# Query and key operands of a hybrid decoder layer: split once over 128 rows, then carried to their rows by transfers

## Chip, core and metric

The kernel runs on one core of one Trainium2 chip. The metric is the device time of one execution in microseconds (us). The core has a matrix engine (TensorE, PE in the profile; PEld is its weight load), a vector engine (VectorE, DVE), a scalar engine (ScalarE, ACT), a general engine (GpSimd, POOL) and a sync engine (SyncE, SP) that here only issues transfers. Every engine works through its own queue of instructions in order and waits on semaphores; transfers (DMA) are issued by an instruction of SP, POOL or ACT and land later.

## What is computed

One inference step of a decoder layer for a prompt of 1024 tokens and 8 decode sequences of 8 tokens (1088 columns in all), with shared weights. Cut to what matters here:

```python
xn = rmsnorm(x, norm1_g)
proj = xn @ w_in
q, k, v, glu_a, glu_b, gate_a, gate_b = split(proj)
attn = sliding_window_attention(q, k, v, sinks)      # window 128, 16 heads over 4 key heads, head size 64
branch_a = attn @ w_o_attn
branch_b = silu(layernorm(causal_dwconv31(glu_a * sigmoid(glu_b)))) @ w_pb
h = x + (sigmoid(gate_a) * branch_a + sigmoid(gate_b) * branch_b) @ w_out
y = h + conv_ffn(rmsnorm(h))                          # then a final rmsnorm
```

Everything is float32 at the outside. Inside, each operand of a matmul is kept as two float32r halves, a rounded high half and the difference to it (low half), and a product is three matmuls: high by high, high by low, low by high.

## The kernel before

**Tiling.** Activations lie with channels on the 128 partitions and tokens along the row. A weight of 128 output channels is a "unit": `stream` (L204) runs it over three chunks of columns (384, 384 and 320; the last has 256 prompt columns and 64 decode columns). A chunk is 8 steps of three matmuls (L200, L201, L202), so 24 matmuls into one PSUM bank; there are four banks of tag `mm` and four of tag `aux`. After a chunk an evacuation function `evac(c, o, n, ps)` reads the bank. The order of the units is the list `SEQUENCE` (L54): `b a q0 g q0 b a q0 q0 k0 b a v v`, then gates, `b`s and `a`s, then `q1 q1 q1 g q1 k1 b a ...`. The first five units are run chunk by chunk side by side with the first normalisation (L832 to L848).

**Queries.** Units `q0` and `q1` hold two heads each (64 rows of one key head g=0, 64 of g=1); four units make a group of four heads for each g. The operand of the scores for key head g is the tile `q{g}` of 128 rows: the rows r of g hold the high half, the other 64 rows x hold the low half. So a single matmul over 128 rows multiplies both halves. `q_evac` (L715) does, per g, an ACT copy of 64 rows into r (L727) and a DVE subtraction of 64 rows into x (L728).

**Keys.** `do_k` (L737) makes `kd{g}` with the high half on both sets of 64 rows and `kl{g}` with the low half on both: per g, ACT writes kd's rows r (L748), DVE writes kl's rows r (L750), and ACT copies both to the rows x (L751, L752).

**Users.** `attn_unit` (L338) reads them in `scores` (L356, L357), for the first group after `v`, for the second from the moment that its keys are there. Its output is written over the columns of `q0`/`q1` that it has read; those of the first group are sent to DRAM by POOL (`attn_spill`, L400), and the second group's queries use the same two tiles (one buffer each).

**Other work beside it.** ACT and DVE split each raw weight into halves (`w_split`, L181 and L182), evacuate the `b`, `a` and gate units, do the softmax and the splits of its transposes (`split_ps`, L228 to L230), and DVE runs the 31-tap convolutions (`conv`, L468; its taps are L480, some 47 long DVE operations per convolution). SP loads raw weights (L158, two buffers `wraw`) and the convolution's history into `u` (L661, two buffers).

**What sets the order.** The code is traced by a framework that tracks reads and writes by region, puts in the semaphores, and orders each engine's queue ahead of time with its own estimates of durations, by priority among what it reckons to be ready. Priority is the order of tracing; `later(off)` lowers it, and the convolutions stand at `later(1200)` (L690), so they fill what DVE has left. At run time each queue is followed strictly. A tile of a pool has as many buffers as its `bufs`; the pools `qp`, `cv` and `gl` have one unless a call says otherwise.

Of the kernel before, what the change touches and what calls it, by code (L numbers as in the profile page):

```python
# [6 lines left out]
F32 = mybir.dt.float32  # L7
F32R = mybir.dt.float32r
AF = mybir.ActivationFunctionType
ALU = mybir.AluOpType  # L10
AX = mybir.AxisListType

P = 128
# [106 lines left out]
class Build:  # L120
# [515 lines left out]
    def pool(self, es, name, side="right", bufs=1):  # L636
        return es.enter_context(self.tc.tile_pool(name=name, bufs=bufs, side=side, reuse_waits="tile"))

    def phase_x(self):
        nc, tc, a, pool = self.nc, self.tc, self.a, self.pool  # L640
# [5 lines left out]
        gl = pool(right, "gl")  # L646
# [56 lines left out]
        def gate_evac(kind, i):  # L703
# [8 lines left out]
                nc.gpsimd.dma_start(dst[i, :, o:o + n], t[:, :n])  # L712
            return ev

        def q_evac(p, j):  # L715
            st = states[p]
            if j == 0:
                st["q"] = [self.t(qp, [P, 4, T], f"q{g}", F32R) for g in range(2)]
                st["qs"] = self.t(qp, [P, NB // 2, 3 * 8 * NT], "qs")
                nc.gpsimd.memset(st["qs"], 0.0)  # L720

            def ev(c, o, n, ps):
                m = min(n, SEQ - o)
                for g in range(2):
                    r, x = [slice(y * HD, (y + 1) * HD) for y in (g, 1 - g)]
                    q = st["q"][g][:, j, o:o + m]
                    nc.scalar.copy(q[r], ps[r, :m])  # L727
                    nc.vector.tensor_tensor(q[x], ps[r, :m], q[r].bitcast(F32), ALU.subtract)  # L728
                if m < n:
                    for g in range(2):  # L730
                        r = slice(g * HD, (g + 1) * HD)
                        row = st["qs"].rearrange("p a (s x) -> p a s x", s=3)[r, :, 0:3:2]
                        nc.scalar.copy(row[:, :, :, (4 * g + j) * NT:(4 * g + j + 1) * NT],
                                       ps[r, m:n].rearrange("p (a s t) -> p a s t", a=NB // 2, s=2))
            return ev

        def do_k(p):  # L737
            st = states[p]
            st["ks"] = self.t(kv, [P, NS], "ks")
            st["kd"] = [self.t(kv, [P, SEQ], f"kd{g}", F32R) for g in range(2)]  # L740
            st["kl"] = [self.t(kv, [P, SEQ], f"kl{g}", F32R) for g in range(2)]

            def ev(c, o, n, ps):
                m = min(n, SEQ - o)
                for g in range(2):
                    r, x = [slice(y * HD, (y + 1) * HD) for y in (g, 1 - g)]
                    kd = st["kd"][g][:, o:o + m]
                    nc.scalar.copy(kd[r], ps[r, :m])  # L748
                    kl = st["kl"][g][:, o:o + m]
                    nc.vector.tensor_tensor(kl[r], ps[r, :m], kd[r].bitcast(F32), ALU.subtract)  # L750
                    nc.scalar.copy(kd[x], ps[r, :m])  # L751
                    nc.scalar.copy(kl[x], kl[r].bitcast(F32))  # L752
                if m < n:
                    nc.scalar.copy(st["ks"], ps[:, m:n])
                    kf = self.t(gl, [P, 384], "gt", bufs=2)[:, :WIN]
                    nc.scalar.copy(kf, ps[:, m - WIN:m])
                    nc.gpsimd.dma_start(a["o_kp"][p], kf)
                    nc.gpsimd.dma_start(a["o_kn"][p], st["ks"])

            self.stream(("k", p), xs, ev)  # L760
# [38 lines left out]
        p0_es = ExitStack()  # L799
        p0 = pool(p0_es, "p0", "left")  # L800
        put_q = [q_evac(0, j) for j in range(2)]
        spare = [q[:, 3, :DM] for q in states[0]["q"]]
        self.slot = lambda i: (None, spare) if i == 4 else (p0, "xy"[i - 2]) if 2 <= i < FIRST else (self.wp, i % 2)
# [60 lines left out]
        for n, (kind, i) in enumerate(self.order[:self.n_in]):  # L864
# [16 lines left out]
            if kind == "b":  # L881
                u = do_b(i)
            elif kind == "a":
                do_a(i, u)
            elif kind in ("ga", "gb"):
                self.stream((kind, i), xs, gate_evac(kind, i))
            elif kind == "q":
                if i == (1, 0):
                    self.drain()
                self.stream((kind, i), xs, q_evac(*i))  # L890
            elif kind == "k":
                do_k(i)
                if i == 1:
                    plan_units(1)
            elif kind == "v":
                if i == 0:
                    do_v()
                    plan_units(0)
# [892 lines left out]
```

## Time and profile before

| | us |
|---|---|
| median of 3 runs | 1660.74 |
| lowest, highest | 1658.13, 1662.14 |
| the profiled execution's own time | 1659.53 |
| its span in the profile | 1657.8 |

In the profile, "busy" of PE counts the modelled length of a matmul, and matmuls overlap: a 384-column matmul is listed with about 0.33 us, but the next one starts well before that. The pace of PE is therefore read from the starts of neighbouring rows, and its stalls from the idle time that a row shows in brackets, `[idle before <-releaser]`. Rows of windows give, for each engine, the busy us and the number of instructions; "PEclk" is the granted clock of PE as a share of full speed. Rows of a line's view give minimum, median and maximum of its durations in ns.

### The profile page before, as it was taken

How to read it: one execution, taken by the hardware profiler on the slowest of the kernel's cores; microseconds unless marked ns; L12 is line 12 of the kernel's file. 1: busy time of each engine (PE TensorE's matmuls, PEld its weight loads, DVE VectorE, ACT ScalarE, POOL GpSimd, SP SyncE). 2: the span in 40 equal slices, each digit the busy share in tenths (PEclk: the TensorE clock that was granted, in tenths of full speed). 3: DMA queues.
4: the chain of work that ended last, by engine and by line, in shares of the span. 5: the costliest groups of instructions: out<-in, count | busy, mean ns of one | idle time of the engine just before them, and what ended most of it. 6: DMA issues, size and time to landing. Idle time of an engine off the chain costs nothing.

```text
span 1657.8 us, 30344 instructions
## 1 busy us (share of the span) xinstructions
PE 1642.9 (99%) x11616; PEld 1627.3 (98%) x11616; DVE 1336.1 (81%) x2430; ACT 893.3 (54%) x1817; POOL 328.1 (20%) x589
## 2 busy tenths in 40 slices
PE   9999999999999999999999999999999999999998
PEld 9999999999999999999999999999999999999997
DVE  8899999999769995866685897877777777977556
ACT  7434477753488754993343564444444446834322
POOL 1210114171211211110000123333433220000050
PEclk9999999999999999999999999999999999999999
DMA  6122216254421255545346527676777544857473
GB/s 213 43 52 71 60 63 167 62 178 103 115 67 47 83 195 184 165 137 190 113 136 194 134 79 204 183 182 176 182 176 176 144 112 149 286 157 218 138 148 117
DMA packets 121313, 232.12 MB, mean 140 GB/s; under 512 B 25408, under 2 KB 67536, under 8 KB 120736
## 3 DMA queue, kind: packets, MB, share of 16 engines
q1 hardware_dynamic: 88208, 140.14, 27.6%
q0 software_dynamic: 32384, 89.51, 21.3%
q8 instruction: 91, 1.49, 0.4%
q10 hardware_dynamic: 576, 0.53, 0.1%
q14 instruction: 54, 0.44, 0.1%
HBM read 169.74 MB, written 89.62 MB: 156 GB/s over the span
## 4 chain that ended last, share of the span: by engine, by line
PE 81%; DVE 11%; ACT 4%; issue 2%; DMA 1%; POOL 0%; SPq 0%; DVEq 0%; ACTq 0%; POOLq 0%
PE mm L200 19%; PE mm L202 19%; PE mm L201 19%; PE aux L200 6%; PE aux L202 6%; PE aux L201 6%; DVE c L480 3%; DVE bt L480 2%; PE aux L366 1%; ACT p L332 1%; ACT p L336 1%; PE aux L378 1%; DVE wlo L182 1%; PE aux L356 1%; PE aux L379 1%
## 5 line engine op out<-in xcount | busy, mean ns | idle before, releaser
L200 PE MATMUL mm<-xh,whi 128*128 128x384 f32 (+1 forms) x920 | 306.6, 333 | 0.6 <-ACT whi L181 0.6
L201 PE MATMUL mm<-xl,whi 128*128 128x384 f32 (+1 forms) x920 | 301.1, 327 | 0.0
L202 PE MATMUL mm<-xh,wlo 128*128 128x384 f32 (+1 forms) x920 | 300.7, 327 | 0.0
L200 PEld LDWEIGHTS mm<-xh,whi 128*128 128x128 f32 x920 | 173.3, 188 | 2.2 <-ACT whi L181 1.2
L201 PEld LDWEIGHTS mm<-xl,whi 128*128 128x128 f32 x920 | 173.4, 188 | 1.0
L202 PEld LDWEIGHTS mm<-xh,wlo 128*128 128x128 f32 x920 | 173.1, 188 | 0.1
L1209 DVE SCALAR_TENSOR_TENSOR acc<-st,fc,acc 128x1104 f32<-128x1104 f32 x88 | 119.5, 1361 | 8.7 <-ACT acc L1207 7.9
L181 ACT CAST whi<-wraw 128x1024 fp32r<-128x1024 f32 (+1 forms) x65 | 62.7, 970 | 56.8 <-PE mm L201 44.6
L480 DVE SCALAR_TENSOR_TENSOR bt<-u,consts,bt 128x513 f32<-128x513 f32 x120 | 89.7, 747 | 0.6
L480 DVE SCALAR_TENSOR_TENSOR c<-sm,hsum,c 128x512 f32<-128x512 f32 x120 | 89.4, 745 | 0.5
L182 DVE TENSOR_TENSOR wlo<-wraw,whi 128x1024 fp32r<-128x1024 f32 (+1 forms) x65 | 72.5, 1121 | 20.1 <-ACT whi L181 19.6
L480 DVE SCALAR_TENSOR_TENSOR c<-u,consts,c 128x512 f32<-128x512 f32 x112 | 83.5, 745 | 0.2
L229 ACT CAST wlo<-th 128x512 fp32r<-128x512 f32 x56 | 35.1, 626 | 65.0 <-PE aux L202 41.3
L1378 ACT COPY st<-mm 128x272 f32<-128x272 f32 (+2 forms) x133 | 44.4, 350 | 46.8 <-PE mm L202 46.8
L200 PE MATMUL mm<-th,whi 128*128 128x272 f32 x240 | 69.3, 289 | 0.0
L202 PE MATMUL mm<-th,whi 128*128 128x272 f32 x240 | 69.3, 289 | 0.0
L201 PE MATMUL mm<-tl,whi 128*128 128x272 f32 x240 | 69.1, 288 | 0.0
L332 ACT ACTIVATE p<-p,nm 128x257 f32<-128x257 f32 (+1 forms) x128 | 62.2, 490 | 11.0 <-DVE nm L327 10.1
L1357 DVE TENSOR_TENSOR st<-st,aux 128x272 f32<-128x272 f32 (+2 forms) x95 | 34.2, 378 | 38.5 <-PE aux L202 38.5
L202 PE MATMUL mm<-sh,wlo 128*128 128x384 f32 (+1 forms) x192 | 62.6, 326 | 0.0
L201 PE MATMUL mm<-sl,whi 128*128 128x384 f32 (+1 forms) x192 | 62.6, 326 | 0.0
L200 PE MATMUL mm<-sh,whi 128*128 128x384 f32 (+1 forms) x192 | 62.6, 326 | 0.0
(651 smaller groups left out, 5906.8 us busy)
## 6 DMA issues: line engine op xcount, KB each, us to landing
wraw<-wall SPq DMA_DIRECT2D x87, 512.0 KB, 4.0
d_x<-st POOLq DMA_DIRECT2D x27, 544.0 KB, 4.9
d_wd<-wall POOLq DMA_DIRECT2D x54, 256.0 KB, 6.1
th<-wall SPq DMA_DIRECT2D x18, 512.0 KB, 6.0
wraw<-wall SPq DMA_DIRECT2D x33, 256.0 KB, 4.1
x<-d_x SPq DMA_DIRECT2D x14, 544.0 KB, 4.8
d_x<-acc POOLq DMA_DIRECT2D x9, 816.0 KB, 7.2
d_wo<-wall POOLq DMA_DIRECT2D x24, 256.0 KB, 4.9
```

The costliest lines, as they stand in the source:

```text
L181: self.nc.scalar.copy(h[:, z], r[:, z])
L182: self.nc.vector.tensor_tensor(l[:, z], r[:, z], h[:, z].bitcast(F32), ALU.subtract)
L200: mm(ps, wh, xh, start=first, stop=False, skip_group_check=more)
L201: mm(ps, wh, xl, start=False, stop=False, skip_group_check=more)
L202: mm(ps, wl, xh, start=False, stop=last, skip_group_check=more)
L229: self.nc.scalar.copy(h, src)
L332: nc.scalar.activation(pt[:, j, lo:width + 1], pt[:, j, lo:width + 1], AF.Exp, bias=nm[:, j:j + 1], scale=-1.0, accum_out=den[:, j:j + 1])
L336: nc.scalar.activation(pt[:, j, lo:width], pt[:, j, lo:width], AF.Identity, scale=den[:, j:j + 1])
L480: mac = lambda o, x, w: nc.vector.scalar_tensor_tensor(o, x, w, o, ALU.mult, ALU.add)
L1209: self.last_tap = nc.vector.scalar_tensor_tensor(acc, st[:, k:k + AW], fw(f, k), acc, ALU.mult, ALU.add)
L1357: plus = lambda d, s: nc.vector.tensor_tensor(d, d, s, ALU.add)
L1378: op(d, r(ps))
```

## The change

The evacuation of a query or key chunk first makes both halves of all 128 rows at once, in two new tiles `qkh` and `qkl` of the pool `gl` (128 x 384, one buffer each): one ACT copy and one DVE subtraction, by `split_ps` (L228). SP then issues transfers of 64 rows each that carry the halves to their rows of the operands: four for a chunk of queries (high and low half, for g = 0 and 1), eight for a chunk of keys (each of high and low to both sets of rows, for g = 0 and 1). The copies of the decode columns (L733) and of the keys' outputs (L754 to L758) stay.

```diff
+        def both_parts(ps, m):
+
+            h, l = [self.t(gl, [P, 384], f"qk{z}", F32R) for z in "hl"]
+            self.split_ps(h[:, :m], l[:, :m], ps[:, :m])
+            return h, l
+
         def q_evac(p, j):
...
                 m = min(n, SEQ - o)
+                parts = both_parts(ps, m)
                 for g in range(2):
                     r, x = [slice(y * HD, (y + 1) * HD) for y in (g, 1 - g)]
                     q = st["q"][g][:, j, o:o + m]
-                    nc.scalar.copy(q[r], ps[r, :m])
-                    nc.vector.tensor_tensor(q[x], ps[r, :m], q[r].bitcast(F32), ALU.subtract)
+                    for z, part in zip((r, x), parts):
+                        nc.sync.dma_start(q[z].bitcast(F32), part[r, :m].bitcast(F32))
...
                 m = min(n, SEQ - o)
+                parts = both_parts(ps, m)
                 for g in range(2):
                     r, x = [slice(y * HD, (y + 1) * HD) for y in (g, 1 - g)]
-                    kd = st["kd"][g][:, o:o + m]
-                    nc.scalar.copy(kd[r], ps[r, :m])
-                    kl = st["kl"][g][:, o:o + m]
-                    nc.vector.tensor_tensor(kl[r], ps[r, :m], kd[r].bitcast(F32), ALU.subtract)
-                    nc.scalar.copy(kd[x], ps[r, :m])
-                    nc.scalar.copy(kl[x], kl[r].bitcast(F32))
+                    for to, part in zip((st["kd"], st["kl"]), parts):
+                        for z in (r, x):
+                            nc.sync.dma_start(to[g][z, o:o + m].bitcast(F32), part[r, :m].bitcast(F32))
```

## The prediction

> **What bounds the kernel now.** I read the page first (busy shares, then the chain), then windows by stage, then the timeline of PE where it stops.
>
> ```profile
> span 1657.8 us, 30344 instructions
> PE 1642.9 (99%) x11616; PEld 1627.3 (98%) x11616; DVE 1336.1 (81%) x2430; ACT 893.3 (54%) x1817; POOL 328.1 (20%) x589
> PE 81%; DVE 11%; ACT 4%; issue 2%; DMA 1%; POOL 0%; SPq 0%; DVEq 0%; ACTq 0%; POOLq 0%
> ```
>
> ```profile
> 0.00:60.00 60.00, 55.62 (x311) 54.54 (x312) 50.12 (x101) 40.36 (x87) 7.38 (x15) 0.97 0.47 151
> 60.00:184.00 124.00, 124.00 (x831) 123.88 (x830) 117.74 (x181) 48.73 (x99) 19.48 (x25) 1.00 0.23 59
> 184.00:345.00 161.00, 158.56 (x1019) 153.51 (x1018) 156.22 (x354) 122.75 (x313) 42.87 (x80) 0.99 0.36 99
> 345.00:452.00 107.00, 107.00 (x652) 106.78 (x651) 96.77 (x148) 39.22 (x78) 38.13 (x52) 1.00 0.51 134
> 452.00:600.00 148.00, 147.65 (x962) 142.87 (x961) 126.97 (x309) 124.05 (x320) 25.73 (x48) 1.00 0.23 65
> 600.00:1657.80 1057.80, 1050.04 (x7852) 1045.69 (x7850) 788.30 (x1342) 518.17 (x924) 194.49 (x370) 1.00 0.58 166
> ```
>
> The chain gives PE 81% and DVE 11%, but the windows say what that DVE share is worth. The six stages are the start, the rest of the first queries and keys up to the values, the first attention, the second queries, the second attention, and the rest. In the two stages that hold nearly all the changed evacuations (60 to 184, 345 to 452) PE is never idle: 124.00 of 124.00 and 107.00 of 107.00 us, although DVE is nearly full (117.74). A faster DVE is worth nothing there as such. PE's idle time up to 600 us is 4.38 + 0 + 2.44 + 0 + 0.35 us; whatever the change can win lies in those 7.2 us and in the slow clock behind a stop.
>
> Two of the stops are ended by DVE and lie behind changed work.
>
> ```profile
> 32.29 1.14 DVE L728 TENSOR_TENSOR q<-qt,q 64x384 fp32r<-64x384 f32 x2 [0.18 <-ACT q L727]
> ...
> 35.51 1.14 DVE L728 TENSOR_TENSOR q<-qt,q 64x384 fp32r<-64x384 f32 x2
> ...
> 48.15 3.98 DVE L274 TENSOR_TENSOR sq<-sq,sq 128x320 f32<-128x320 f32 x7
> 52.06 0.17 DVE L311 RECIPROCAL rows<-rows 128x3 f32<-128x3 f32 x1
> ...
> 52.28 0.93 PE L296 MATMUL aux<-consts,rows 128*128 128x128 f32 x6 [1.46 <-DVE rows L311]
> ```
>
> First, at 52.28 PE has waited 1.46 us for the row sums of a normalisation. Between 32.29 and the reciprocal at 52.06 the DVE timeline shows no idle bracket, so what is taken out of DVE at 32.29 and 35.51 brings the reciprocal forward.
>
> ```profile
> 200.26 0.58 ACT L229 CAST pth<-aux 128x512 fp32r<-128x512 f32 x1
> ...
> 202.79 0.68 DVE L230 TENSOR_TENSOR ptl<-aux,pth 128x512 fp32r<-128x512 f32 x1
> ...
> 203.52 0.38 PE L356 MATMUL aux<-kd,q 128*128 128x256 f32 x1 [2.15 <-DVE ptl L230]
> ...
> 204.33 0.49 PE L356 MATMUL aux<-kd,q 128*128 128x256 f32 x1
> ...
> 207.51 0.51 PE L201 MATMUL mm<-xl,whi 128*128 128x384 f32 x1
> 207.83 0.36 PE L202 MATMUL mm<-xh,wlo 128*128 128x384 f32 x1
> ...
> 209.07 0.33 PE L200 MATMUL mm<-xh,whi 128*128 128x384 f32 x1
> 209.24 0.33 PE L201 MATMUL mm<-xl,whi 128*128 128x384 f32 x1
> ```
>
> Second, at 203.52 PE has waited 2.15 us for the low half of a transposed probability block. ACT had its half done at 200.84, and DVE, full of convolution taps, came to it at 202.79, 1.95 us late. After the stop, from 204.33 to 207.83, matmuls start 0.32 us apart (207.51, 207.83) instead of 0.17 (209.07, 209.24): 3.5 x (1 - 0.17/0.32) = 1.64 us more is lost to a halved clock.
>
> The Trainium skill, page "TensorE: Matmul & The Clock Gate", section "Why this matters for your kernels", asks for no idle gap of PE over about 3 us; by it a gap of 2.15 us would cost 2.15 us and no clock. The rows above differ: the slow stretch follows the gap, and the measurement decides. By the page the faster rival below would be 1656.2 us and count as no change.
>
> **The change part by part.**
>
> ```profile
> L727 ACT CAST q<-mm x36: 367/474/481, 104.1 to 443.9; 64x384 fp32r<-64x384 f32 x24, 64x256 fp32r<-64x256 f32 x12
> L728 DVE TENSOR_TENSOR q<-mm,q x36: 417/552/560, 107.5 to 444.3; 64x384 fp32r<-64x384 f32 x24, 64x256 fp32r<-64x256 f32 x12
> L748 ACT CAST kd<-mm x12: 366/474/478, 132.0 to 456.0; 64x384 fp32r<-64x384 f32 x8, 64x256 fp32r<-64x256 f32 x4
> L750 DVE TENSOR_TENSOR kl<-mm,kd x12: 416/550/561, 133.0 to 456.6; 64x384 fp32r<-64x384 f32 x8, 64x256 fp32r<-64x256 f32 x4
> L751 ACT CAST kd<-mm x12: 352/472/477, 133.6 to 458.1; 64x384 fp32r<-64x384 f32 x8, 64x256 fp32r<-64x256 f32 x4
> L752 ACT CAST kl<-kl x12: 403/512/514, 134.0 to 458.5; 64x384 fp32r<-64x384 f32 x8, 64x256 fp32r<-64x256 f32 x4
> L709 ACT COPY gt<-mm x45: 400/462/494, 196.9 to 647.1; 128x384 f32<-128x384 f32 x30, 128x320 f32<-128x320 f32 x15
> L827 DVE TENSOR_TENSOR qt<-mm,rstd x5: 480/547/551, 30.6 to 79.0; 128x384 f32<-128x384 f32 x3, 128x320 f32<-128x320 f32 x2
> ```
>
> Removed: 128 rows cost what 64 rows cost (ACT 0.462 against 0.474, DVE 0.547 against 0.552), so a 384-column query chunk loses one ACT copy of 0.47 and one DVE subtraction of 0.55. Over 16 such chunks and 8 of 256 columns (0.42 by the minimum of L728) DVE is spared 16 x 0.55 + 8 x 0.42 = 12.2 us. Keys spare DVE 4 x 0.55 + 2 x 0.42 = 3.0 us, and ACT five of six copies a chunk. Of DVE's 15.2 us almost all falls where PE is not waiting: worth 0, covered by PE's own matmuls (if that cover were gone, PE idle at every chunk, it would be worth at most the 15.2 us). What counts lies in front of the two stops:
>
> - At 52.28: each of the two rows with x2 (1.14 us) is halved, so the reciprocal comes 2 x 0.57 = 1.14 us earlier, and the 1.46 us shrink to 0.3, where the squares themselves are late. Minus 1.14 us. Bounds: 0 (if the planner puts other work into the hole) to 1.46.
> - At 203.52: before it DVE is spared 12 query chunks and 3 key chunks, 10 x 0.55 + 5 x 0.42 = 7.6 us. But the convolutions fill every hole, and nothing in the views shows that their taps would stand elsewhere relative to `ptl`. I take 0; bounds: minus 2.15 - 1.64 = -3.8 us, or as much again on the other side if the new order puts another such stop.
>
> Added: 24 x 4 + 6 x 8 = 144 transfers of 64 rows on SP's queue, 64 x 384 x 4 bytes = 96 KB at most, 12.6 MB in all, and a wait: ACT may overwrite `qkh`, and DVE `qkl`, only when the transfers of the chunk before have landed.
>
> ```profile
> L158 SPq DMA_DIRECT2D wraw<-wall x83: 327/328/642, 12.6 to 1355.4; - x83
> ...
> d_ga<-gt POOLq DMA_DIRECT2D x16, 192.0 KB, 2.2
> xr<-xT SPq DMA_DIRECT2D x32, 136.0 KB, 3.3
> wraw<-wall SPq DMA_DIRECT2D x87, 512.0 KB, 4.0
> ...
> SPq L158 <- DVE wlo L182: 509.9, 43, 41.2
> SPq L661 <- DMA d_c<-u: 67.7, 8, 21.7
> ```
>
> An issue takes SP 0.33 us, so 144 take 47 us of a queue that spends 509.9 us waiting for weight buffers: worth 0. No row is a transfer from SBUF to SBUF. The nearest are 2.2 us (out of SBUF, 192 KB), 3.3 us (into SBUF on SP's queue, 136 KB) and 4.0 us (a whole weight). I take 2.2, the one that also starts in SBUF beside matmuls; the 3.3 rows lie in the crowded load of the start.
>
> A query chunk then holds its pair for 0.55 (subtraction) + 4 x 0.33 + 2.2 = 4.1 us; PE makes a chunk in 24 x 0.17 = 4.1 us. A key chunk holds it 0.55 + 8 x 0.33 + 2.2 = 5.4 us, 1.3 more than PE's pace, 3.9 us over three chunks. What waits behind the blocked ACT copy and DVE subtraction are weight halves (L181, L182), other evacuations and taps. PE feels it when all four `mm` banks are full, that is after three chunks or 12.3 us of lag. So 3.9 us cost 0.
>
> ```profile
> 445.47 0.47 ACT L748 CAST kd<-mm 64x384 fp32r<-64x384 f32 x1 [0.25 <-PE mm L202]
> ...
> 452.94 0.28 PE L356 MATMUL aux<-kd,q 128*128 128x256 f32 x1
> ```
>
> The closest user is the second attention: its first scores start at 452.94, and the key chunk they read is begun at 445.47. By the new way it is there at 445.47 + 0.47 + 0.55 + 8 x 0.33 + 2.2 = 451.3, 1.6 us early: 0. With 4.0 us of landing it would be 0.2 us late, which PE would wait. The first attention has tens of us.
>
> **Sum** against the profiled execution's own 1659.53 us (span 1657.8 and 1.73 around it; 1.2 below the median of 1660.74): -1.14 + 0 + 0 = 1658.4 us. That is no change: 0.3% of the median, about what a measurement can tell, is 5.0 us, so "same" is 1655.8 to 1665.7.
>
> **The rivals.**
>
> Faster: the 7.6 us of DVE do reach `ptl`, and the stop at 203.52 goes with its slow clock. For it: DVE is busy 117.74 of 124 us before, so its lateness there was gathered over that stretch. Against: the taps are in the queue whichever way. 1659.53 - 1.14 - 3.79 = 1654.6 us. Chance 0.2.
>
> Slower, the single pair: if transfers land later than assumed, the pair, not PE, sets the pace. At 4.0 us a query chunk takes 5.9 (lag 1.8) and a key chunk 7.2 (lag 3.1). The run q0 q0 k0 gathers 6 x 1.8 + 3 x 3.1 = 20.1, less 12.3 is 7.8 us of PE stop; q1 q1 q1 gathers 9 x 1.8 = 16.2, so 3.9; a gate unit drains it, then q1 k1 5.4 + 9.3 = 14.7, so 2.4. Together 14.1: 1672.5 us. It decides from where six query and three key lags pass 12.3, a landing of about 3.2 us. For it: 3.3 and 4.0 in rows of the same queue; against: 2.2. Chance 0.2.
>
> Slower, SP's order: SP follows its queue, and history loads (L661) waited in it up to 21.7 us for a convolution. Query transfers behind such a load wait with it, and the pair with them: 21.7 + 4 x 0.33 + 2.2 - 12.3 = 12.9 us at worst, 1671 us; at the mean wait of 67.7 / 8 = 8.5 it is covered. With it I count a new stop in the attention of the kind at 203.52, 1659.53 - 1.14 + 3.79 = 1662.2, which would still be "same". Chance of over 5 us: 0.12.
>
> **How the numbers follow.** Same 0.48 (1658.4, its own range 1655.8 to 1665.7), faster 0.2, slower 0.32. For 8 in 10 the range must reach the faster rival and the two slower ones: 1653.5 to 1672.5, which leaves outside a gain at both stops and beyond (about 0.05) and landings later than 4 us (about 0.13).
>
> **What would show it.** Right: L296 near 52 us with an idle of some 0.3 us; transfers out of `qkh` and `qkl` landing in about 2.2 us; windows 60 to 184 and 345 to 452 with PE still never idle; first scores of the second attention without idle in front of them. Wrong: ACT L229 or DVE L230 idle for a DMA out of `qkh` or `qkl`, growing from chunk to chunk, followed by PE idle at an `mm` bank; SP waiting at L661 with query transfers behind; or the stop at 203 gone or doubled.

## The result and the profile after

| | us |
|---|---|
| before, median of 5 runs | 1660.45 (1658.13 to 1662.14) |
| after, median of 5 runs | 1675.32 (1673.53 to 1675.97) |
| ratio | 1.0087, 95% interval 1.0075 to 1.0098 |
| profiled execution of after, its own time | 1675.33 (span 1673.6) |

The changed kernel is slower by 14.9 us. The forecast was 1658.4 and no change, and the range ended at 1672.5. The two profiled executions differ by 1675.33 - 1659.53 = 15.8 us; the profiles are read against that number.

The page of after, its span, busy times and the shares of the chain that ended last:

```profile
span 1673.6 us, 30569 instructions
PE 1645.7 (98%) x11616; PEld 1628.3 (97%) x11616; DVE 1316.2 (79%) x2400; ACT 867.5 (52%) x1763; POOL 328.9 (20%) x589
...
PE 80%; DVE 10%; DMA 4%; ACT 3%; issue 2%; SPq 1%; POOL 0%; DVEq 0%; ACTq 0%; POOLq 0%
```

DVE's busy time fell by 1336.1 - 1316.2 = 19.9 us and ACT's by 25.8, so the change did take the work off both. The time nevertheless grew. What is new in the chain is DMA, from 1% to 4%.

The windows of after by the same stages (PE, PEld, DVE, ACT and POOL as busy us and count, then PEclk, DMA share, GB/s):

```profile
60.00:184.00 124.00, 124.00 (x834) 124.00 (x834) 112.30 (x173) 36.48 (x73) 19.24 (x29) 1.00 0.40 104
...
345.00:452.00 107.00, 106.10 (x640) 104.87 (x639) 86.17 (x132) 28.21 (x53) 39.21 (x54) 1.00 0.60 160
452.00:600.00 148.00, 136.69 (x873) 132.04 (x872) 112.43 (x279) 109.05 (x285) 23.34 (x44) 0.95 0.31 86
```

The first group's stage (60 to 184) still has PE busy for all of its 124.00 us. The loss stands in one row: from 452 to 600 PE is idle for 11.31 us, where before it was idle for 0.35, and the clock is 0.95 instead of 1.00. The timeline of PE (start, duration, line, operation, and in brackets the idle time and what ended it) shows where:

```profile
50.48 0.93 PE L296 MATMUL aux<-consts,rows 128*128 128x128 f32 x6 [0.67 <-DVE rows L311]
...
203.13 0.58 PE L356 MATMUL aux<-kd,q 128*128 128x256 f32 x1 [3.01 <-DVE ptl L230]
...
208.53 0.52 PE L202 MATMUL mm<-xh,wlo 128*128 128x384 f32 x1
208.85 0.48 PE L200 MATMUL mm<-xh,whi 128*128 128x384 f32 x1
...
451.40 0.42 PE L200 MATMUL mm<-xh,whi 128*128 128x320 f32 x1 [0.82 <-DVE qkl L230]
...
463.97 0.55 PE L356 MATMUL aux<-kd,q 128*128 128x256 f32 x1 [8.79 <-DMA kd<-qkh]
466.71 0.55 PE L357 MATMUL aux<-kl,q 128*128 128x256 f32 x1 [2.19 <-DMA kl<-qkl]
...
471.54 0.52 PE L201 MATMUL mm<-xl,whi 128*128 128x384 f32 x1
471.86 0.40 PE L202 MATMUL mm<-xh,wlo 128*128 128x384 f32 x1
```

PE stands 8.79 + 2.19 = 10.98 us in front of the first two scores of the second attention, waiting for the key transfers. From 466.71 to 471.86 the matmuls are 0.32 us apart as behind the stop at 203.52 before (the granted clock from 467.0 to 471.8 is 0.50), which costs 5.15 x (1 - 0.17/0.32) = 2.4 us. The stop at 203 grew by 0.86, and the slow stretch behind it, from the next matmul at 203.51 to 208.85, is 5.3 us long instead of 3.5, which costs 1.8 x (1 - 0.17/0.32) = 0.8 more. A stop at a full `mm` bank costs 0.82, and the stop near 52 us shrank by 0.79. That is 10.98 + 2.4 + 0.86 + 0.8 + 0.82 - 0.79 = 15.1 of the 15.8 us. The other 0.7 was not traced to a place. The first 60 us hold several small stops that differ between the two profiles: although the stop near 52 us shrank, PE's idle time there went from 4.38 to 4.86 us.

Why are the keys late? The timeline of ACT over the last chunks in front of the scores (the casts at L229 into `qkh` are the start of each evacuation):

```profile
436.17 0.48 ACT L229 CAST qkh<-mm 128x384 fp32r<-128x384 f32 x1
...
449.71 0.48 ACT L229 CAST qkh<-mm 128x384 fp32r<-128x384 f32 x1 [13.06 <-DMA q<-qkh]
...
456.06 0.37 ACT L229 CAST qkh<-mm 128x256 fp32r<-128x256 f32 x1 [4.92 <-DMA q<-qkh]
...
459.13 0.48 ACT L229 CAST qkh<-mm 128x384 fp32r<-128x384 f32 x1 [0.53 <-DMA q<-qkh]
464.31 0.48 ACT L229 CAST qkh<-mm 128x384 fp32r<-128x384 f32 x1 [4.71 <-DMA kd<-qkh]
```

These are the three query chunks of the last `q1` and the first two key chunks. Each of the last four waits for the transfers of the chunk before, because there is one `qkh`. The longest wait, 13.06 us, has its reason on SP, whose timeline (an issue's start and its duration) reads:

```profile
439.50 0.33 SPq L158 DMA_DIRECT2D wraw<-wall  x1
443.67 0.60 SPq L661 DMA_DIRECT2D u<-cbT  x1
444.36 1.50 SPq L735 DMA_DIRECT2D q<-qkh  x2
445.95 1.19 SPq L735 DMA_DIRECT2D q<-qkl  x2
...
459.63 2.38 SPq L757 DMA_DIRECT2D kd<-qkh  x4
```

The high half of the first chunk was in `qkh` at 436.17 + 0.48 = 436.65. SP came to its transfers at 444.36, 7.7 us later, because a weight load and a history load stood in front of them in its queue and were waiting for their own buffers. The transfers then took until 449.7 to land, and only then could ACT go on. Their landing in this stretch, from the view of L735 between 435 and 480 us:

```profile
L735 SPq DMA_DIRECT2D q<-qkh x6: 462/588/857, 444.4 to 457.0; - x6
...
DMA to landing us min/median/max: 1.9/4.5/5.8
```

### The profile page after: what moved, and what is told of

Same layout as the page of the kernel before. It is cut to its first block, busy times and chain, and to the rows that moved or that the text cites. A ratio compares the mean times of both kernels' runs of the same rounds, so it can differ in the third digit from the quotient of the medians.

```text
span 1673.6 us, 30569 instructions
## 1 busy us (share of the span) xinstructions
PE 1645.7 (98%) x11616; PEld 1628.3 (97%) x11616; DVE 1316.2 (79%) x2400; ACT 867.5 (52%) x1763; POOL 328.9 (20%) x589
## 4 chain that ended last, share of the span: by engine, by line
PE 80%; DVE 10%; DMA 4%; ACT 3%; issue 2%; SPq 1%; POOL 0%; DVEq 0%; ACTq 0%; POOLq 0%
PE mm L200 18%; PE mm L201 18%; PE mm L202 18%; PE aux L200 6%; PE aux L202 6%; PE aux L201 6%; DVE c L480 3%; DMA q<-qkl 2%; DVE bt L480 2%; PE aux L366 1%; DMA q<-qkh 1%; DMA d_c<-u 1%; PE aux L378 1%; DVE wlo L182 1%; PE aux L356 1%
## 5 line engine op out<-in xcount | busy, mean ns | idle before, releaser
L332 ACT ACTIVATE p<-p,nm 128x257 f32<-128x257 f32 (+1 forms) x128 | 62.2, 489 | 14.9 <-DVE nm L327 14.1
L229 ACT CAST wlo<-th 128x512 fp32r<-128x512 f32 x56 | 35.1, 626 | 65.3 <-PE aux L202 41.6
```

Source lines behind the costliest of these rows:

```text
L229: self.nc.scalar.copy(h, src)
L332: nc.scalar.activation(pt[:, j, lo:width + 1], pt[:, j, lo:width + 1], AF.Exp, bias=nm[:, j:j + 1], scale=-1.0, accum_out=den[:, j:j + 1])
```

## The experiments

The first theory was the single pair, made worse by SP's order: one staging pair makes chunk follow chunk by a whole round trip, and SP's queue lengthens the trip where another load waits in front. The first rival was SP's order alone, with the pair harmless. A second rival was contention with the weight folds, that is, with DMA traffic. A third was that the work removed or the new order of the queues shifts stops elsewhere. Each time stands as a ratio to runs of the kernel before on the same chip.

**The first group alone.** The first group keeps the new way, the second group (p = 1) takes the old one, for queries and for keys (the same branch stands around the transfers of `do_k`).

```diff
-                parts = both_parts(ps, m)
+                if p:
...
+                        nc.scalar.copy(q[r], ps[r, :m])
+                        nc.vector.tensor_tensor(q[x], ps[r, :m], q[r].bitcast(F32), ALU.subtract)
+                else:
+                    parts = both_parts(ps, m)
```

> Queries and keys of the second group by the old way, of the first group by the new one. If the whole loss is the stop of 8.8 + 2.2 us in front of the second group's first scores and the slow clock behind it (13.3 us more lost at 460 to 480 than before), this gives 1659 to 1662 us and no idle in front of those scores. If a part of the loss is spread over the first group (transfers beside everything, the stop at 203), it stays over 1664.

Measured: 1659.49 us, ratio 0.9999 (0.9990 to 1.0008). The whole loss belongs to the second group, and what the first group saves on DVE and ACT is worth nothing that can be measured.

**The history load on POOL's queue.** This takes one of the two loads in front of the query transfers out of SP's queue.

```diff
-            nc.sync.dma_start(u_views(u)[:, :, 0:HIST], a["cbT"][i])
+            nc.gpsimd.dma_start(u_views(u)[:, :, 0:HIST], a["cbT"][i])
```

> The changed kernel with the convolution's history loads issued by POOL and not by SP. Theory 'order': the loss comes from query transfers that stood in SP's queue behind a history load until 444.4 us, 7.7 us after their half was ready; then the wait for kd falls from 8.8 to 1 to 3 us and the time to 1664 to 1668. Theory 'pair': the single pair's round trip is above PE's pace in any case and fills the whole slack; then the wait stays at 6 us or more and the time at 1672 to 1676.

Measured: 1673.23 us, ratio 1.0080 (1.0064 to 1.0097), that is 2.1 us less than after by the medians, with intervals that overlap. PE's waits (us in total, times, longest) name the same place, smaller:

```profile
PE aux L356 <- DMA kd<-qkh: 6.3, 1, 6.3
```

SP's timeline shows why so little came of it:

```profile
429.78 9.35 SPq L158 DMA_DIRECT2D wraw<-wall  x2
439.22 1.13 SPq L735 DMA_DIRECT2D q<-qkh  x2
```

The weight load in front of the history load still holds the queue: the issues begin at 439.22, 3.5 us after the half was ready at 435.74 (its ACT copy starts at 435.25 and takes 0.49), where it was 7.7 us in after. So this run takes only a part of SP's wait away. It shows that the history load is not the cause by itself while the pair is single.

**Two pairs for the second group.** Once the pool of values is open, the pair is allocated there with two buffers.

```diff
+        where = [gl, 1]
+
...
-            h, l = [self.t(gl, [P, 384], f"qk{z}", F32R) for z in "hl"]
+            own, n = where
+            h, l = [self.t(own, [P, 384], f"qk{z}", F32R, bufs=n) for z in "hl"]
...
+        where[:] = kv, 2
```

> The changed kernel with two pairs of staging tiles after the first phase (in the pool kv), the queues as they are. Theory 'pair': the split no longer waits for the chunk before; the wait for kd falls to 2 us or less, 1660 to 1665. Theory 'order': the transfers still wait in SP's queue behind the history load; the wait falls by one chunk's round trip at most, to 4 to 5 us, 1668 to 1671.

Measured: 1663.3 us, ratio 1.0016 (1.0005 to 1.0027). A second pair takes 1675.32 - 1663.3 = 12.0 of the 14.9 us away (by the ratios, 0.71% of 0.87%). PE's waits still hold the place:

```profile
PE aux L356 <- DMA kd<-qkh: 3.2, 1, 3.2
```

and SP's timeline still has the history load in front of the transfers:

```profile
437.84 0.60 SPq L661 DMA_DIRECT2D u<-cbT  x1
438.53 1.26 SPq L738 DMA_DIRECT2D q<-qkh  x2
```

The half was ready at 432.67 + 0.48 = 433.15 by ACT's timeline and went out 5.4 us later. So a remainder hangs on SP's order.

**Both.** Two pairs, and the history load on POOL's queue.

> Two pairs and history loads on POOL together. Both theories: no wait of more than 2 us in front of the second group's scores, 1659 to 1663. If 3 us or more are left, it is the eight key transfers and their landing themselves, which stand between the last split and the scores.

Measured: 1658.01 us, ratio 0.9987 (0.9978 to 0.9996). The window of the second attention is what it was before the change:

```profile
452.00:600.00 148.00, 147.65 (x958) 142.89 (x958) 127.27 (x310) 120.65 (x314) 24.94 (x47) 1.00 0.25 73
```

PE's timeline has the first scores without an idle bracket, and ACT's has no wait for a DMA in front of these chunks:

```profile
450.93 0.35 PE L356 MATMUL aux<-kd,q 128*128 128x256 f32 x1
```

```profile
431.59 0.48 ACT L229 CAST qkh<-mm 128x384 fp32r<-128x384 f32 x1 [2.96 <-PE mm L202]
435.75 0.48 ACT L229 CAST qkh<-mm 128x384 fp32r<-128x384 f32 x1 [3.68 <-PE mm L202]
440.07 0.36 ACT L229 CAST qkh<-mm 128x256 fp32r<-128x256 f32 x1
443.50 0.48 ACT L229 CAST qkh<-mm 128x384 fp32r<-128x384 f32 x1 [1.27 <-issue]
447.65 0.48 ACT L229 CAST qkh<-mm 128x384 fp32r<-128x384 f32 x1 [3.68 <-PE mm L202]
```

These are the same five chunks as in after. There they take 464.31 - 436.17 = 28.14 us from the first to the fifth, here 447.65 - 431.59 = 16.06, and ACT waits for PE's matmuls, as it should. The first key chunk, the fourth row, starts 459.13 - 443.50 = 15.6 us earlier than in after, and the first scores start 463.97 - 450.93 = 13.0 us earlier.

**Folds later.** The folds of the output weights (L613, with DMA traffic of their own) are moved behind the stretch.

```diff
-FOLD_FROM = 12
+FOLD_FROM = 32
...
-                    self.fold(next(out_folds, ()))
+                    for _ in range(2):
+                        self.fold(next(out_folds, ()))
```

> The changed kernel, single pair and SP's order as they are, with the weight folds on POOL (transfers from DRAM to DRAM, one stage a unit from unit 12 to 35) started at unit 32, two stages a unit, so that none runs beside the second group's queries. Theory 'crowd': the transfers out of the pair land late there (median 4.5 us at 435 to 480, 2.2 at 380 to 435) because folds and a convolution's store fill the DMA engines; then they land in 2.2 to 2.5 us, the wait for kd falls to 3 us or less, 1662 to 1667. Theory 'pair and order alone': the history load and the round trip remain; wait over 6 us, 1671 to 1676.

Measured: 1673.11 us, ratio 1.0083 (1.0068 to 1.0098). PE's waits changed more than the time did:

```profile
PE aux L521 <- DVE red L514: 4.3, 2, 2.5
PE aux L356 <- DMA kd<-qkh: 3.2, 1, 3.2
PE aux L357 <- DMA kl<-qkl: 2.2, 1, 2.2
```

In front of the scores 5.4 us are left of 10.98, and 4.3 us of new stops appear later, at 656.33 and 664.69. The landing is the one that the theory 'crowd' expected:

```profile
L735 SPq DMA_DIRECT2D q<-qkh x6: 461/588/1137, 441.2 to 448.9; - x6
...
DMA to landing us min/median/max: 1.9/2.2/4.8
```

The DMA engines were busy for 0.94 of the time from 442 to 458 us in after, and for 0.62 from 441 to 456 here, where the same chunks lie. So the folds' traffic did make the transfers land late, and it is a third part of the lag. The total hides this, because the new stops took back most of what was won; that the moved folds caused those stops was not shown. The folds are not the whole cause either: ACT still waited 10.59 us for one query transfer, since the history load left SP at 440.51, with the transfers behind it. After that the query chunks followed each other in 3.27 and 3.07 us (casts at 444.76, 448.03 and 451.10), faster than PE's 4.1. With a free queue and less traffic even the single pair keeps up with query chunks.

**Queries new, keys old**, and **keys new, queries old**: each half of the change by itself.

```diff
-                            nc.sync.dma_start(to[g][z, o:o + m].bitcast(F32), part[r, :m].bitcast(F32))
+                    nc.scalar.copy(kd[r], ps[r, :m])
...
```

> Queries by transfers, keys by the six ACT copies and two DVE subtractions of before. Theory 'lag of the queries': the first key chunk's evacuation no longer waits for the pair, as it needs none, and the scores wait only for the last query chunks, which lie 9 us of PE ahead; 1659 to 1664 us with at most 2 us of wait. Theory 'blocked engine': ACT still stands in its queue at the last query chunks (13.1 and 4.9 us in the profile), the keys' copies behind it are as late, and the scores wait 3 to 6 us; 1665 to 1670.

> Queries as before, keys by transfers. If eight transfers of some 0.59 us and a landing of 2.2 are themselves too long for the place in front of the scores, the wait for kd is 2 us or more, 1662 to 1666. By the estimate of the prediction (there 1.6 us early with an issue of 0.33; with 0.59 it is 2 us later, 0.5 us late) it is 0 to 1 us: 1659 to 1662.

Measured: 1669.04 us with the old keys, ratio 1.0058 (1.0041 to 1.0075), and 1665.97 with the old queries, 1.0041 (1.0026 to 1.0056). With the old keys there is no key transfer at all, and PE still stands in front of the scores:

```profile
PE aux L356 <- ACT kd L758: 5.5, 1, 5.5
```

ACT's timeline of that kernel shows what delayed this copy:

```profile
445.31 0.48 ACT L229 CAST qkh<-mm 128x384 fp32r<-128x384 f32 x1 [13.30 <-DMA q<-qkh]
...
454.61 0.47 ACT L755 CAST kd<-mm 64x384 fp32r<-64x384 f32 x1
```

ACT was blocked 13.30 us by the query transfers, and the keys, which do not use the pair, stood in ACT's queue behind it. So a stop that the profile puts down to a key is here the debt of the queries. With the old queries PE waits only 0.44 + 0.35 + 0.67 us at the scores, between the two estimates, though the time lies at the end of the worse one. The profiled execution of that kernel is 1664.54, 5.0 above the one before; the rest of its loss is spread and was not settled.

**Transfers on ACT's queue** instead of SP's (`nc.scalar.dma_start` in both places).

> The changed kernel with the transfers issued on ACT's queue: nothing of SP stands in front of them, and an issue costs ACT some 0.5 us, 2 to 4.7 us a chunk. Theory 'order': the history load is no longer in the way, wait for kd at most 4 us, 1662 to 1667. Theory 'pair': ACT issues the low half only after DVE's subtraction and so stands still itself; the round trip is as long as before, 1670 to 1680.

Measured: 1678.57 us, ratio 1.0113 (1.0098 to 1.0128). They no longer stand behind weight and history loads, but they stand in the queue of the engine that makes the halves. PE's waits:

```profile
PE aux L356 <- DMA kd<-qkh: 7.0, 1, 7.0
...
PE mm L200 <- ACT gt L761: 4.5, 1, 4.5
```

The stop at the scores shrank from 10.98 to 7.0 + 1.3 us, but new stops at full `mm` banks appeared: the 4.5 us stand at 152.58, in the first group's stage, and 0.85 and 1.75 us in the second's (421.81 and 435.66). ACT's queue is no remedy while the pair is single. POOL's queue was not tried for these transfers.

**A gate unit between the keys and their scores.** The gate unit in front of the last `q1` is moved behind `k1`, so that 12 us of PE work lie between the keys and the attention.

```diff
-    "q1 q1 q1 g q1 k1 b a g b a g g g g g g g"
+    "q1 q1 q1 q1 k1 g b a g b a g g g g g g g"
...
+                if self.order[n - 1] == ("k", 1):
+                    plan_units(1)
...
-                if i == 1:
-                    plan_units(1)
```

> The changed kernel with the gate unit that stood between the second group's queries moved behind its keys, and the second attention started after that gate unit: the scores stand at the same place of PE's queue, but the last query and key chunks are 12 us of PE ahead of them. Theory 'place of the scores': the lag of the evacuations is as long as before, but nobody waits for it at the scores; wait for kd at most 1 us, 1660 to 1665; what is left would be a stop at a full bank inside the longer run of 15 chunks, 2 to 6 us if the lag passes 12.3 us. Theory 'banks': the lag costs PE wherever it is; 1670 or more.

Measured: 1674.97 us, ratio 1.0092 (1.0078 to 1.0106). PE's timeline:

```profile
443.86 0.44 PE L200 MATMUL mm<-xh,whi 128*128 128x384 f32 x1 [0.98 <-ACT qs L740]
...
451.02 0.44 PE L200 MATMUL mm<-xh,whi 128*128 128x384 f32 x1 [2.71 <-DVE qkl L230]
...
459.68 0.28 PE L356 MATMUL aux<-kd,q 128*128 128x256 f32 x1
...
463.94 0.69 PE L200 MATMUL mm<-xh,whi 128*128 128x384 f32 x1 [3.17 <-ACT gt L761]
```

The first scores, at 459.68, no longer wait, and nothing is won: the stops moved to the banks. They are 0.98 + 2.71 + 3.17 us and one more of 0.59 at 456.06, and from 464.43 to 469.65 the matmuls are 0.32 us apart again. The lag is not an effect of where the scores stand; it is paid at the first user that cannot go on without the chunk.

**Controls.** The kernel before with the history load on POOL's queue, then "both" once more, then "both" with the gate unit moved.

> A control: the kernel before with its history loads on POOL's queue, nothing else. If the gain of the run with two pairs and history loads on POOL (0.9987) comes from the history loads alone, this gives the same 0.998 to 0.999; if it comes from the new evacuation, this gives 1.000 within 0.001.

> Two pairs and history loads on POOL again, on the same chip as the control: 1657 to 1659 us, ratio 0.998 to 0.999.

> Two pairs, history loads on POOL and the gate unit behind the keys. With no wait left in front of the scores in either order, the move of the gate unit is worth nothing: 1656 to 1660 us. If the order of the units costs something by itself, over 1661.

Measured: 1660.97 us, ratio 1.0008 (0.9999 to 1.0017), for the control; 1658.42, 0.9989 (0.9980 to 0.9998), for "both" on another chip; 1658.18, 0.9988 (0.9979 to 0.9997), with the gate moved. So the history load gives nothing without the change, and the change with two pairs and a free queue is some 0.11 to 0.13% faster than before. That is less than the 0.3% that the forecast counted as a difference, but three measurements agree on it.

## Why the prediction was wrong

**The bound (right).** PE bounds the kernel, and DVE's relief is worth nothing where PE is not waiting: DVE was spared 19.9 us (15.2 were forecast), the first group's stage kept PE at 124.00 of 124.00 us, and the kernel with the new first group alone has a ratio of 0.9999.

**The stop at 52.28 (right in kind).** It shrank from 1.46 to 0.67 us instead of 0.3, a gain of 0.79 instead of 1.14. The kernels with the old queries in the first group keep a stop of 1.5 to 1.6 us there, and all with the new queries have 0.7 or less. It does not show in the time.

**The stop at 203.52 (inside its bounds).** Taken as no change; it went from 2.15 to 3.01 us. In the other kernels it lay between 0.7 and 3.0 us (0.77 and 0.71 in the two profiles of "both", 2.98 with the gate unit alone); only the kernel with the transfers on ACT's queue, which stops for 4.5 us at 152.58, has none there. What sets it was not settled; the faster rival, which needed it gone, did not come.

**The pair's round trip (the step that failed).** The prediction charged "0.55 (subtraction) + 4 x 0.33 + 2.2 = 4.1 us" for a query chunk, set that against PE's 4.1 and concluded "So 3.9 us cost 0". Three things in it were wrong.

- The sizes. The issue was taken from a weight load's row. The rows of the new transfers, over the whole kernel of after, say:

```profile
L735 SPq DMA_DIRECT2D q<-qkh x48: 461/547/1252, 31.6 to 457.0; - x48
...
L757 SPq DMA_DIRECT2D kd<-qkh x24: 461/587/1201, 129.4 to 475.8; - x24
```

 An issue takes 0.55 to 0.59 us, not 0.33, and the landing in the stretch that counts takes 4.5, not 2.2, because of the folds' traffic. The forecast had named 3.2 us of landing as the point from which the pair decides. ACT's rows in after show what a chunk took, from cast to cast: 449.71 - 436.17 = 13.54 us for the first of the last three query chunks, 6.35 for the second and 3.07 for the third, where 4.1 was charged; a key chunk took 464.31 - 459.13 = 5.18, where 5.4 was charged. So the excess lies in two query chunks: 13.54 + 6.35 - 2 x 4.1 = 11.7 us. Of these, 7.7 are the wait in SP's queue, and the other 4.0 are about two landings that were each taken 2.3 us too short. The longer issue alone did no harm, as the 3.27 and 3.07 us with the folds moved show.

- The queue in front of it. SP's waits were called worth 0 for the transfers and made into a separate rival. On the chip they add to the same round trip: 7.7 us between the ready half and its first issue. What they cost depends on the pair: by the medians, moving the history load saves 2.1 us with one pair (with intervals that overlap) and 1663.3 - 1658.0 = 5.3 us with two.

- The place of payment. The lag was charged against three free `mm` banks (12.3 us), and the second attention was checked with a key chunk begun at 445.47 as before. But the banks hide the lag only from the chunks that PE makes next. The scores read the keys themselves, so they wait for the whole lag that has gathered: the first key chunk began at 459.13, not 445.47, and PE, which had reached its scores at 452.94 before, got to them at 463.97.

The Trainium skill, page "Trainium Kernel Development and Optimization", section "Best Practices", asks for double buffers so that transfers and compute overlap. This case agrees: the second pair alone is worth 12.0 us. The Trainium skill, page "DMA: Bandwidth & Descriptors", section "Anatomy of one DMA — SWDGE (gpsimd) path", fits 2.0 us plus the bytes over 436 KB a us, an estimate of 2.2 us for 96 KB. The transfers of after, on SP's queue, agree from 380 to 435 (median 2.2 us) and disagree where it mattered (4.5 from 435 to 480).

**The rivals.** "Slower, the single pair" had the right mechanism and nearly the size, 14.1 us at a landing of 4.0 against 14.9 measured. That the size agrees is luck: it laid all stops at the banks, 7.8 us of them in the first group, where nothing was lost, and none at the scores, where nearly all was lost. "Slower, SP's order" was the other part of the same trip. The two were treated as alternatives, each with a chance of its own, and the range ended at the larger of them; but they happen together, and the time came out 2.8 us beyond it.

## What to carry to other kernels

A staging tile with one buffer puts the whole round trip (evacuate, wait for a place in the issuing queue, issue, land) between two chunks; compare that trip, with the longest wait of that queue and the landing of the busiest stretch in it, with the pace of the engine that feeds it, and give the tile two buffers unless it is clearly shorter. Free banks behind it hide a lag only from the producer: look up who reads the last chunk, and start that reader's sum from the delayed chunk, not from the time in the old trace. When the stop turns up at the reader, ask which earlier chunk began the delay, since work that never used the tile can stand blocked behind it in the same engine's queue.

## What was not expected of the hardware

- A transfer of 64 rows from SBUF to SBUF holds SP for 0.46 us at least and 0.55 to 0.59 in the median, against a median of 0.33 for a weight load of 512 KB. The issue did not follow the bytes: the weight loads that stand right behind such transfers in after, at 457.65 and 471.53, took 0.54 and 0.53 us.
- Its landing depends on the traffic beside it more than on its size: a median of 2.2 us from 380 to 435 and 4.5 from 435 to 480, in one kernel, and 2.2 from 435 to 480 with the folds moved. In "both", with the folds where they were, the median from 435 to 480 was 6.2 us, and nothing waited for it at the scores.
- The slow clock behind a stop does not follow the length of the gap alone. Before the change a gap of 2.15 us was followed by 3.5 us at a pitch of 0.32; in after 3.01 us by 5.3 us, and the 8.79 and 2.19 us in front of the scores by 5.15 us. With the gate unit moved, a gap of 2.71 us, at 451.02, was followed by the full pitch of 0.17 us (451.31, 451.48). With two pairs and the history load on SP's queue the gap at the scores was 3.23 us, and PE's timeline has the pitch of 0.17 to 0.18 us in the very next unit:

```profile
455.39 0.35 PE L356 MATMUL aux<-kd,q 128*128 128x256 f32 x1 [3.23 <-DMA kd<-qkh]
...
456.64 0.34 PE L200 MATMUL mm<-xh,whi 128*128 128x384 f32 x1
456.82 0.34 PE L201 MATMUL mm<-xl,whi 128*128 128x384 f32 x1
```

 The Trainium skill, page "TensorE: Matmul & The Clock Gate", section "Why this matters for your kernels", puts the limit at gaps of about 3 us. These runs have slow stretches behind gaps on both sides of it, and gaps without one on both sides; on what it depends stays open.
